# The input projections of a hybrid attention layer in five units of seven block products, with all of the attention half in one fixed list of steps

## The chip, the cores and the metric

The kernel runs on one core of a Trainium2 chip. A core has a matrix engine (TensorE, PE in the profile, with its weight loads as PEld), a vector engine (VectorE, DVE), an activation engine (ScalarE, ACT), GpSimd (POOL) and a queue engine (SyncE, SP), each with its own in-order queue of instructions, and 16 DMA engines between the chip's memory and the core's SBUF. TensorE writes its results to PSUM; the other engines read them there. Engines wait for each other by semaphores. The metric is the time of one execution on the device, in microseconds, as the median of several runs.

## The reference

One layer on 256 tokens of width 2048, in float32:

```
h    = rms_norm(x, attn_norm)
qa, ka, va, fa, qb, kb, vb = split(h @ w_in)     # 1024 each, fa 8 columns
qa, ka = rms_norm per head of 128
c    = cumsum(log_sigmoid(fa + b_forget))
out_a = softmax(qa ka^T / sqrt(128) + c_t - c_s, s <= t) va      # 8 heads
out_b = stick-breaking attention(qb, kb, vb), s < t               # 8 heads
x    = x + concat(rms_norm(out_a), rms_norm(out_b)) @ w_out
u    = causal conv of width 3 (rms_norm(x) @ w_up)                # 2 x 5632 columns
x    = x + (silu(gate half of u) * value half of u) @ w_down
```

Weights in all are some 200 MB, each used once, so every weight tile is loaded, prepared and used in one pass.

## The kernel before

Products keep float32 accuracy through a split. Of each operand a high part (`w_hi`, a cast on ACT, L208) and the rest (`w_lo`, a subtraction on DVE, L209) are made, and three products are summed: high by high, low of the tokens by high, high by low (`in_three`, L222 to L232, its matmul is L229). A weight piece is 2048 columns a partition: 4 tiles of 128 contraction rows by 512 columns, `w_raw`, 1 MB, loaded by SP.

The attention half is ordered by a scheduler that follows data and priorities. Ten projections of 512 columns read the normalised tokens `hT`: the forgetting heads' q and k, in two halves each (`project`, token-major, 4 pieces of 24 matmuls); the stick-breaking q and k in two halves each (`sb_heads`, feature-major, 16 pieces, L261 and L266); and the stick-breaking v in two halves. The forgetting heads' v and the 8 gate columns are three more projections of 344 columns. The first projection runs with the loading and the transposing of x (`opening`). Token-major q and k are turned into heads by transposes on TensorE (`ps_h`, L301) after a norm whose squares and sums are taken on DVE (`fox_rows`, L315, L317). The feature-major ones need no transposes, but the token factors `rstd1` in every partition (`pr`, L181). Heads are generators in a queue, `waiting`, of which each piece of a projection advances two. A head is a few small matmuls (`ps_s` or `ps_z`, `ps_p`, `ps_o`), exponentials on ACT, and masks and maxima on DVE. `w_out` is 16 pieces in two groups of 8, one for each kind of head; a column block of it is finished, added to x (L575), before the next begins. PSUM is in three pools of two: `psa` tiles of two banks, `psb` and `pss` of one.

The feed-forward half, from about 409 us on, is a list of steps in a fixed order, written out at the end of the function: at each step, weights for six steps ahead are loaded, those for four ahead summed, those for two ahead split, and the step's matmuls run. Its up-projection alternates with the down-projection of an earlier part; the down-projection takes seven block products in place of eight (`down_in_seven`), with banks `bank_a`, `bank_b` and `bank_c` as tiles of their own, and a buffer of its own for the sums of weights, `w_sum` (L781).

Of the kernel before, what the change touches and what calls it, by code (L numbers as in the profile page):

```python
# [14 lines left out]
P = 128  # L15
# [22 lines left out]
AHEAD = 200  # L38
WINDOW = 2
# [4 lines left out]
def hybrid_layer(  # L44
# [26 lines left out]

    const = ctx.enter_context(tc.tile_pool(name="const", bufs=1))
    big = ctx.enter_context(tc.tile_pool(name="big", bufs=1))
    small = ctx.enter_context(tc.tile_pool(name="small", bufs=4))
    psa = ctx.enter_context(tc.tile_pool(name="psa", bufs=2, space=bass.MemoryType.PSUM))
    psb = ctx.enter_context(tc.tile_pool(name="psb", bufs=2, space=bass.MemoryType.PSUM))

# [8 lines left out]
    x2 = big.tile([P, NT, D], F32, name="x2")  # L86
    xt = [x2[:, t, :] for t in range(NT)]
    xp = xf.rearrange("(t p) d -> p t d", p=P)

    def load_x(k, n):  # L90
        nc.sync.dma_start(x2[:, :, k * P : (k + n) * P], xp[:, :, k * P : (k + n) * P])

    with tc.high_priority(offset=AHEAD):
        load_x(0, 2)
        nc.sync.dma_start(cs[:, :P], cst[:, :P])
        nc.sync.dma_start(prow[:KT, :], attn_norm[0].rearrange("(n p) -> n p", p=P))
# [4 lines left out]
    ones = cs[:, C_ONE : C_ONE + P]  # L101

# [3 lines left out]
    def load_parameters(masks):  # L106
# [21 lines left out]


    pcol = const.tile([P, 50], F32, name="pcol")  # L130
    ga = const.tile([P, KT], F32, name="ga")
    g_ffn = pcol[:, KT : 2 * KT]
    g_fox, g_sb = pcol[:, 2 * KT : 2 * KT + NH], pcol[:, 2 * KT + NH : 2 * KT + 2 * NH]
    g_q, g_k = pcol[:, 48:49], pcol[:, 49:50]
# [6 lines left out]
    hT = big.tile([P, KT, 2, S], F32R, name="hT")  # L141

    def transposed_split(k, g):

        ps = psb.tile([P, 2, S], F32, name="ps_x", tag="t")
        for j in range(2):
            for t in range(NT):
                nc.tensor.transpose(  # L148
                    ps[:, j, t * P : (t + 1) * P], xt[t][:, (k + j) * P : (k + j + 1) * P], ident
                )  # L150
        for j in range(2):
# [7 lines left out]
    def sums_of_squares(ss, c):  # L159

        for t in range(NT):
            junk = late.tile([P, 512], F32, name="junk", tag="raw", bufs=4)
            act.activation(junk, xt[t][:, c * 512 : (c + 1) * 512], AF.Square, accum_out=ss[:, t, c : c + 1])

    def token_factors(ss, n):

        rstd = const.tile([P, NT], F32, name=f"rstd{n}")
        ssum = small.tile([P, NT], F32, name="ssum", tag="ssum")
        dve.tensor_reduce(ssum, ss, axis=AX.X, op=ALU.add)
        rsqrt(rstd, ssum, 1.0 / D, NT)  # L170
        dg = []
        for t in range(NT):
            dg.append(small.tile([P, P], F32, name="dg", tag="dg", bufs=2))
            dve.tensor_scalar(dg[t], ident, rstd[:, t : t + 1], None, op0=ALU.mult)
        return rstd, dg

    def in_every_partition(dg, n, pool):
        R = pool.tile([P, S], F32, name=f"R{n}")
        pr = psb.tile([P, S], F32, name="pr", tag="t")
        for t in range(NT):  # L180
            nc.tensor.matmul(pr[:, t * P : (t + 1) * P], ones, dg[t], start=t == 0, stop=t == NT - 1)  # L181
        dve.tensor_copy(R, pr)
        return R


    waiting = deque()

    def step():
        for g in list(waiting)[:WINDOW]:
            if next(g, g) is g:  # L190
                waiting.remove(g)

    def finish():
        while waiting:
            step()


    def load(src, into=None):
        raw = into if into is not None else wraw.tile([P, 2048], F32, name="w_raw", tag="w_raw")
# [15 lines left out]
    def weights(src, a, b):  # L215
        with tc.high_priority(offset=AHEAD):
            return split(load(src), a, b)

# [3 lines left out]
    def in_three(accs, parts, n, lhs, starts, stops):  # L222

# [3 lines left out]
        for j, (i, l, r) in enumerate(order):  # L227
            for t, o in enumerate(accs):
                nc.tensor.matmul(  # L229
                    o, lhs(i, l, t), r[:, i, :], start=starts and j == 0,  # L230
                    stop=stops and j == 3 * n - 1, skip_group_check=len(accs) == 1 and not starts,
                )  # L232

# [3 lines left out]
    def token_major(lhs, w, k0, nk, c0, cols, pieces=None, before=None):  # L237

        acc = psa.tile([P, NT, 512], F32, name="acc", tag="acc")
        k = 0  # L240
        for n in pieces or [4] * (nk // 4):
            if before:
                before(k, n)
            parts = weights(rows_of(w, k0 + k, n, c0, cols), n, cols)
            in_three(
                [acc[:, t, :cols] for t in range(NT)], parts, n,
                lambda i, part, t: of_half(lhs(k + i), part, t), k == 0, k + n == nk,
            )
            k += n
            step()  # L250
        return acc

    def feature_major(w, c0, pool, tag):

        acc = pool.tile([P, 2, 512], F32, name="pu", tag=tag)
        for kh in range(2):
            hi, lo = weights(rows_of(w, 8 * kh, 8, c0, 2 * P), 8, 2 * P)
            for i in range(8):
                k = 8 * kh + i
                for j in range(2):  # L260
                    nc.tensor.matmul(  # L261
                        acc[:, j, :], hi[:, i, j * P : (j + 1) * P],
                        hT[:, k].rearrange("p a b -> p (a b)"), start=k == 0, stop=False,
                    )
                for j in range(2):
                    nc.tensor.matmul(  # L266
                        acc[:, j, S:], lo[:, i, j * P : (j + 1) * P], hT[:, k, 0, :],
                        start=False, stop=k == KT - 1,
                    )
            step()  # L270
        return acc

    def summed(pool, acc, tag, **kw):

        t2 = pool.tile([P, 2, S], F32, name="t2", tag=tag, **kw)
        with tc.high_priority(offset=2 * AHEAD):
            act.copy(t2, acc[:, :, S:])
            dve.tensor_tensor(t2, acc[:, :, :S], t2, op=ALU.add)
        return t2

    with ExitStack() as actx:

        at = actx.enter_context(tc.tile_pool(name="at", bufs=1))
        pss = actx.enter_context(tc.tile_pool(name="pss", bufs=2, space=bass.MemoryType.PSUM))
        tmp = actx.enter_context(tc.tile_pool(name="tmp", bufs=2))
        wraw = actx.enter_context(tc.tile_pool(name="wraw", bufs=3))
        whi = actx.enter_context(tc.tile_pool(name="whi", bufs=2))
        wlo = actx.enter_context(tc.tile_pool(name="wlo", bufs=2))
        late = actx.enter_context(tc.tile_pool(name="late", bufs=1))

        def project(c0, cols, **kw):
            return token_major(lambda k: hT[:, k], wi, 0, KT, c0, cols, **kw)

        def scaled(dst, ps, t):
            act.activation(dst, ps, AF.Identity, scale=rstd1[:, t : t + 1])

        def to_heads(dst, rows, t, scale):

            ps = psb.tile([P, 4, P], F32, name="ps_h", tag="t")
            for h in range(4):  # L300
                nc.tensor.transpose(ps[:, h, :], rows[:, h * HD : (h + 1) * HD], ident)  # L301
            act.activation(dst[:, :, t * P : (t + 1) * P], ps, AF.Identity, scale=scale)

        def fox_rows(acc, dst, g):

            rows = []
            for t in range(NT):
                raw = late.tile([P, 512], F32, name="raw", tag="raw", bufs=4)
                scaled(raw, acc[:, t, :], t)
                rows.append(raw)  # L310
            for t in range(NT):
                raw = rows[t]
                r3 = raw.rearrange("p (h d) -> p h d", h=4)
                sq = late.tile([P, 512], F32, name="sq", tag="raw", bufs=4)
# [634 lines left out]
```

## Time and profile before

| | us |
|---|---|
| median of 3 runs | 1131.53 (1131.24 to 1132.13) |
| span of the profiled execution, first to last instruction | 1129.0 |
| TensorE busy | 1114.8 |
| VectorE busy | 843.3 |
| ScalarE busy | 680.6 |
| GpSimd busy | 20.9 |

The profiled execution's span lies 2.5 us under the median of the runs; what lies around it is not in the profile. In the rows quoted below, `L229` is line 229 of the kernel, `out<-in` are the program's tile names, and `xN` is a count. Matmuls are pipelined, so a group of them is read from its start to the next group's start. Of all the idle time, TensorE has 14 us, most of it at the two ends.

### The profile page before, as it was taken

Reading aid. Unit: us, or ns where it says so; the run is one execution under the profiler, and the core shown is the slowest. Engines: PE = TensorE matmul, PEld = TensorE weight load, DVE = VectorE, ACT = ScalarE, POOL = GpSimd, SP = SyncE. Lnnn points to the kernel's source line nnn. Section 1 sums busy time; section 2 is a strip of 40 time slices with the busy share of each in tenths; the row PEclk is TensorE's granted clock in tenths of the full one; section 3 lists DMA queues with packets and bytes.
Section 4 is the critical chain, followed back from the end, with each engine's and each line's share of the span. In section 5 each row is a group of like instructions: output and inputs, shape, how many; then the busy total and the mean of one; then the engine's idle time right before and its main releaser. Section 6 shows DMA issues by size and latency. Waiting matters only on the chain.

```text
span 1129.0 us, 14661 instructions
## 1 busy us (share of the span) xinstructions
PE 1114.8 (99%) x5890; PEld 956.6 (85%) x5890; DVE 843.3 (75%) x873; ACT 680.6 (60%) x840; POOL 20.9 (2%) x20
## 2 busy tenths in 40 slices
PE   7999999999999999999999999999999999999998
PEld 6998888888888888888888888888888888888886
DVE  4646656646556666766699898989989798989983
ACT  5644444445664566666667667766776667766751
POOL 0000000000000000000000000000000000000000
PEclk9999999999999999999999999999999999999999
DMA  7766555555444486555649697687949797696951
GB/s 234 219 206 218 171 158 159 185 159 178 149 149 150 149 256 199 188 190 192 195 144 252 220 268 249 187 265 195 290 149 242 240 252 242 188 288 182 291 172 66
DMA packets 170989, 228.17 MB, mean 202 GB/s; under 512 B 3992, under 2 KB 117802, under 8 KB 170922
## 3 DMA queue, kind: packets, MB, share of 16 engines
q1 hardware_dynamic: 162474, 210.47, 57.7%
q0 software_dynamic: 8448, 16.78, 8.6%
q8 instruction: 46, 0.75, 0.3%
q14 instruction: 21, 0.17, 0.0%
HBM read 225.14 MB, written 2.10 MB: 201 GB/s over the span
## 4 chain that ended last, share of the span: by engine, by line
PE 97%; DVE 1%; DMA 1%; ACT 0%; issue 0%; SPq 0%; DVEq 0%; ACTq 0%
PE pu L714 29%; PE acc L229 26%; PE pu L719 15%; PE bank_a L229 10%; PE pu L261 5%; PE bank_b L229 4%; PE pu L266 3%; PE bank_c L229 1%; DVE w_lo L209 1%; PE ps_x L148 1%; DMA x<-in_x_dram 0%; DMA w_raw<-in_w_up_dram 0%; PE ps_h L301 0%; ACT w_hi L208 0%; PE ps_z L511 0%
## 5 line engine op out<-in xcount | busy, mean ns | idle before, releaser
L209 DVE TENSOR_TENSOR w_lo<-w_raw,w_hi 128x2048 fp32r<-128x2048 f32 (+2 forms) x204 | 449.6, 2206 | 196.7 <-ACT w_hi L208 193.4
L208 ACT CAST w_hi<-w_raw 128x2048 fp32r<-128x2048 f32 (+2 forms) x204 | 376.0, 1843 | 248.5 <-PE acc L229 79.6
L714 PE MATMUL pu<-hT,w_hi 128*128 128x512 f32 x1408 | 441.7, 395 | 0.0
L719 PEld LDWEIGHTS pu<-hT,w_lo 128*128 128x128 f32 x1408 | 263.8, 188 | 65.8 <-DVE w_lo L209 4.6
L719 PE MATMUL pu<-hT,w_lo 128*128 128x256 f32 x1408 | 277.6, 278 | 0.9 <-DVE w_lo L209 0.9
L714 PEld LDWEIGHTS pu<-hT,w_hi 128*128 128x128 f32 x1408 | 218.8, 189 | 4.7
L229 PE MATMUL acc<-w_hi,hT 128*128 128x512 f32 (+1 forms) x640 | 143.3, 374 | 0.0
L229 PEld LDWEIGHTS acc<-w_hi,hT 128*128 128x128 f32 x640 | 114.2, 190 | 16.8
L261 PE MATMUL pu<-hT,w_hi 128*128 128x512 f32 x256 | 81.4, 399 | 0.0
L644 ACT ACTIVATE tap<-up,ccol 128x256 f32<-128x256 f32 x176 | 74.6, 495 | 0.0
L229 PE MATMUL acc<-w_lo,hT 128*128 128x512 f32 (+1 forms) x320 | 74.3, 371 | 0.0
L229 PEld LDWEIGHTS acc<-w_lo,hT 128*128 128x128 f32 x320 | 57.8, 189 | 8.7
L209 DVE TENSOR_TENSOR w_lo<-w_sum,w_hi 128x2048 fp32r<-128x2048 f32 x24 | 54.9, 2287 | 12.9 <-ACT w_hi L208 12.9
L208 ACT CAST w_hi<-w_sum 128x2048 fp32r<-128x2048 f32 x24 | 45.8, 1909 | 22.4 <-PE pu L714 20.0
L266 PEld LDWEIGHTS pu<-hT,w_lo 128*128 128x128 f32 x256 | 48.1, 188 | 11.4
L266 PE MATMUL pu<-hT,w_lo 128*128 128x256 f32 x256 | 50.4, 278 | 0.0
L229 PE MATMUL bank_a<-w_hi,g 128*128 128x512 f32 x192 | 47.0, 390 | 0.0
L229 PE MATMUL acc<-w_hi,oT 128*128 128x512 f32 x192 | 46.3, 393 | 0.0
L229 PEld LDWEIGHTS acc<-w_hi,oT 128*128 128x128 f32 x192 | 35.4, 188 | 7.0
L229 PEld LDWEIGHTS bank_a<-w_hi,g 128*128 128x128 f32 x192 | 34.5, 188 | 6.1
L261 PEld LDWEIGHTS pu<-hT,w_hi 128*128 128x128 f32 x256 | 39.0, 189 | 0.0
L637 ACT ACTIVATE gate<-up,ccol 128x256 f32<-128x256 f32 x44 | 24.0, 593 | 18.4 <-DVE up L630 18.4
(177 smaller groups left out, 1098.8 us busy)
## 6 DMA issues: line engine op xcount, KB each, us to landing
w_raw<-in_w_up_dram SPq DMA_DIRECT2D x88, 1024.0 KB, 9.9
w_raw<-in_w_down_dram SPq DMA_DIRECT2D x44, 1024.0 KB, 5.2
w_raw<-in_w_in_dram SPq DMA_DIRECT2D x36, 1024.0 KB, 5.3
w_raw<-in_w_out_dram SPq DMA_DIRECT2D x16, 1024.0 KB, 5.3
w_raw<-in_w_in_dram SPq DMA_DIRECT2D x12, 688.0 KB, 4.9
w_raw<-in_w_down_dram POOLq DMA_DIRECT2D x8, 1024.0 KB, 12.4
w_sum<-in_w_down_dram POOLq DMA_DIRECT2D x8, 1024.0 KB, 9.0
w_raw<-in_w_in_dram SPq DMA_DIRECT2D x8, 512.0 KB, 6.3
```

Of the source, the lines that this page charges most:

```text
L148: nc.tensor.transpose(ps[:, j, t * P : (t + 1) * P], xt[t][:, (k + j) * P : (k + j + 1) * P], ident)
L208: act.copy(hi[:, :n], raw[:, :n])
L209: dve.tensor_tensor(lo[:, :n], raw[:, :n], f32(hi[:, :n]), op=ALU.subtract)
L229: nc.tensor.matmul(o, lhs(i, l, t), r[:, i, :], start=starts and j == 0, stop=stops and j == 3 * n - 1, skip_group_check=len(accs) == 1 an ...
L261: nc.tensor.matmul(acc[:, j, :], hi[:, i, j * P : (j + 1) * P], hT[:, k].rearrange("p a b -> p (a b)"), start=k == 0, stop=False,)
L266: nc.tensor.matmul(acc[:, j, S:], lo[:, i, j * P : (j + 1) * P], hT[:, k, 0, :], start=False, stop=k == KT - 1,)
L637: act.activation(a[:, j, :], u[:, j, 2:], AF.Identity, scale=ccol[:, 2, f : f + 1], bias=ccol[:, 3, f : f + 1],)
L644: act.activation(taps[w][:, j, :], u[:, j, w : w + S], AF.Copy, scale=ccol[:, w, f : f + 1])
L714: nc.tensor.matmul(acc[:, j, :], hi[:, i, j * P : (j + 1) * P], hT[:, k].rearrange("p a b -> p (a b)"), start=k == 0, stop=False,)
L719: nc.tensor.matmul(acc[:, j, S:], lo[:, i, j * P : (j + 1) * P], hT[:, k, 0, :], start=False, stop=k == KT - 1,)
```

## The change

The attention half gets a list of steps too, and the two lists become one: every instruction of PE, DVE, ACT and SP in the whole kernel now stands in the order in which the list issues it. Lines here are those of the kernel after.

- **Opening and values.** The forgetting heads' v comes first: two blocks of 344 columns together, in 8 pieces with the loading of x (`opening`), then the third block in 4 (`last_values`), followed by the gates.
- **Five units.** The ten projections of 512 columns go in pairs, two column blocks n = 0 and 1 to a unit: A and B the forgetting q and k, C the stick-breaking q and k of the first half, V the stick-breaking v, D the q and k of the second half. With two token blocks t = 0 and 1, a unit has four results. For the first 1024 rows of the contraction it takes seven products of blocks in place of eight, 12 matmuls each, on sums of token blocks (made once, `token_sums`) and on sums of weight blocks (two by DVE, two by accumulating DMAs on POOL). For the other 1024 rows it takes four plain pieces of 24. That makes 11 steps. Its four PSUM banks are two tiles: `acc_ac` holds banks a and c, `acc_be` holds b and e. Partial results leave the banks several times in a unit, scaled by `rstd1` (evictions on ACT, L516 and L535; additions on DVE, L522).
- **Heads.** All q and k rows are token-major now, with transposes for the stick-breaking ones. The squares of the forgetting rows move from DVE to ACT: 16 activations of 128 columns with a sum (L577), eight to a tick.
- **x** gives its place to the token sums and is loaded a second time by four DMAs on POOL (`reload_x`) during unit D.
- **w_out.** The second group begins with the first halves of two column blocks, then their second halves.
- **Pools.** Five raw, three high and three low weight buffers throughout; `w_sum` is gone, as the sums are made in place.

The unit:

```diff
+    def unit(c_first, c_second, dst, done):
...
+            def matmuls():
+                if name == "a" and new:
+                    acc = acc_tile("acc_ac")
+                    bank["a"], bank["c"] = acc[:, 0, :], acc[:, 1, :]
+                if name == "b" and new:
+                    acc = acc_tile("acc_be")
+                    turn[0] ^= 1
+                    bank["b"], bank["e"] = acc[:, 0, :], acc[:, 1, :]
+                in_three([bank[name]], parts, 4, lhs, new, True)
...
+        def evict(name, n, t, negative=False):
+            def follow():
+                if not out:
+                    out.update(dst())
+                act.activation(out[n, t], bank[name], AF.Identity, scale=r(t, negative))
+                yield
...
+        def finish():
+            act.activation(out[0, 1], bank["a"], AF.Identity, scale=r(1))
+            yield
+            add("c", 0, 0)
+            yield
+            yield from done(out)
+
+        product("a", True, of_raw(0, 0), "11", [("11", w11)], follow=evict("a", 0, 0))
+        product("c", True, of_raw(1, 0), "21", [("21", w21)])
+        product("b", True, of_sums(T5), "11", [("12", w12)], sum_of("12"), follow=evict("b", 1, 1))
+        plain(1, 0, [(1, "e"), (0, "b")])
+        product("a", False, of_sums(S2), "11", [("22", w22)], sum_of("22"), follow=evict("a", 1, 0, True))
+        plain(1, 1, [(1, "e"), (0, "b")], then_add(("e", 1, 1)))
+        product("a", False, of_sums(T7), "12", plus=w22, follow=then_add(("a", 1, 1, True)))
+        product("b", False, of_sums(S4), "22", follow=then_add(("b", 1, 0)))
+        plain(0, 0, [(0, "c"), (1, "a")])
+        product("a", False, of_raw(1, 1), "11", plus=w21)
+        plain(0, 1, [(1, "a"), (0, "c")], finish)
```

The squares, the order of `w_out` and the list's loop:

```diff
-                dve.tensor_tensor(sq, raw, raw, op=ALU.mult)
...
-                dve.tensor_reduce(ss, sq.rearrange("p (h d) -> p h d", h=4), axis=AX.X, op=ALU.add)
...
+            for m, nt in enumerate(order):
+                for h in range(4):
+                    act.activation(
+                        junk[:, :HD], rows[nt][:, h * HD : (h + 1) * HD], AF.Square,
+                        accum_out=ss[:, m, h : h + 1],
+                    )
+                if m % 2:
+                    yield
...
+    for c in range(4):
+        for kh in range(2):
+            out_rows(0, c, kh)
+    for c, kh in ((0, 0), (1, 0), (0, 1), (1, 1), (2, 0), (2, 1), (3, 0), (3, 1)):
+        out_rows(1, c, kh)
...
     for n in range(-LOAD, len(steps) + 8):
...
+        at_step(LOAD, 0)
+        advance(following)
+        at_step(SPLIT, 2)
+        advance(following)
+        advance_heads()
+        at_step(SUM, 1)
+        at_step(0, 3)
+        advance(after)
+        advance_heads()
```

More of the change, by code (lines that the diff above doesn't have):

```diff
@@ L157, in transposed_split, with squares @@
             )
-    def sums_of_squares(ss, c):
+    def squares(ss, c):
         for t in range(NT):
[L162 to L167, printed above, removed]
+            act.activation(
+                junk, x2[:, t, c * 512 : (c + 1) * 512], AF.Square, accum_out=ss[:, t, c : c + 1]
+            )
@@ L168, in token_factors @@
+    def token_factors(rstd, ss):
         ssum = small.tile([P, NT], F32, name="ssum", tag="ssum")
         dve.tensor_reduce(ssum, ss, axis=AX.X, op=ALU.add)
[L170 to L183, printed above, removed]
@@ L186, in hybrid_layer @@
[L186 to L199, printed above, removed]
+        yield from rsqrt(rstd, ssum, 1.0 / D, NT)
+    steps, following, after, waiting, running = [], [], [], deque(), []
+    hooks = {}
+    ticks = [0, -STAGGER]
@@ new lines, in hybrid_layer, with new_step, advance, advance_heads @@
+    turn = [0]
+    def new_step(load, sums, prepare, matmuls, follow=None):
+        steps.append((load, sums, prepare, matmuls, follow))
+    def advance(tasks):
+        tasks[:] = [g for g in tasks if next(g, g) is not g]
+    def advance_heads():
+        ticks[0] += 1
+        if waiting and ticks[0] - ticks[1] >= STAGGER:
+            running.append(waiting.popleft())
+            ticks[1] = ticks[0]
+        advance(running)
+    def acc_tile(name, slot=None):
+        if slot is None:
+            slot = turn[0]
+            turn[0] ^= 1
+        return psa.tile([P, 2, 512], F32, name=name, tag=f"acc{slot}")
@@ L200, in load @@
+    def load(src):
+        raw = wraw.tile([P, 2048], F32, name="w_raw", tag="w_raw")
         a, b = src.shape[1:]
@@ L234, in of_half, with of_tokens, pieces, loads @@
     def of_half(h, part, t):
         return h[:, part, t * P : (t + 1) * P]
[L237 to L244, printed above, removed]
+    def of_tokens(k0):
+        return lambda i, part, t: of_half(hT[:, k0 + i], part, t)
+    def pieces(w, k0, n, c0, cols, matmuls, follow=None):
+        mem = {}
+        def loads():
+            mem["raw"] = load(rows_of(w, k0, n, c0, cols))
+        def prepare():
+            mem["parts"] = split(mem["raw"], n, cols)
+        new_step(loads, None, prepare, lambda: matmuls(mem["parts"]), follow)
@@ new lines, in sb_rows, with done, start_sb, value_rows @@
+    def sb_rows(half):
+        def done(rows):
+            while started["fox"] < NH or started["sb"] < 4 * half:
+                yield
+            yield from to_heads(rows, (f"qB{half}", f"kB{half}"), (QSCALE, 1.0))
+            ready.add(f"qB{half}")
+            if "vB" in ready:
+                start_sb(half)
+        return done
+    ready = set()
+    def start_sb(half):
+        for h in range(4 * half, 4 * half + 4):
+            waiting.append(sb_head(h, half))
+    def value_rows():
+        tile_of["vB"] = row_tiles("vB")()
+        return tile_of["vB"]
@@ new lines, in norm_of_heads @@
+    def norm_of_heads(group, rg):
+        pg = psb.tile([P, NT], F32, name="pg", tag="t")
+        for t in range(NT):
+            nc.tensor.matmul(
+                pg[:, t : t + 1], ssq[group][:, t * P : (t + 1) * P], ones[:, 0:1],
+                start=t == 0, stop=t == NT - 1,
+            )
+        yield
+        yield from rsqrt(rg, pg, 1.0 / WF, NT)
+        ready.add(f"rg{group}")
+    rgs = [const.tile([P, NT], F32, name=f"rg{i}") for i in range(2)]
+    rstd2 = const.tile([P, NT], F32, name="rstd2")
@@ new lines, in next_rows, with rows_split, out_rows, matmuls @@
+    def next_rows(c):
+        pairs = [(k, transposed(k)) for k in (4 * c, 4 * c + 2)]
+        following.append(rows_split(pairs))
+        yield
+    def rows_split(pairs):
+        for k, ps in pairs:
+            split_tokens(ps, k, g_ffn)
+            yield
+    cells = {}
+    def out_rows(group, c, kh):
+        def matmuls(parts):
+            if kh == 0:
+                cells[c] = acc_tile("acc_o")
+            if group == 1 and kh == 1:
+                while waiting or running:
+                    advance_heads()
+            heads = [hT[:, 4 * kh + i] for i in range(4)] if group == 0 else oSb[4 * kh : 4 * kh + 4]
@@ new lines, in matmuls, with follow @@
+                lambda i, p, t: of_half(heads[i], p, t), kh == 0, kh == 1, middle=middle,
+            )
+            if kh == group and c == 0:
+                following.append(norm_of_heads(group, rgs[group]))
+        def follow():
+            acc = cells[c]
+            while f"rg{group}" not in ready:
+                yield
+            for t in range(NT):
+                xs = x2[:, t, c * 512 : (c + 1) * 512]
+                dve.scalar_tensor_tensor(
+                    xs, acc[:, t, :], rgs[group][:, t : t + 1], xs, op0=ALU.mult, op1=ALU.add
+                )
+            if group == 1:
+                after.append(next_rows(c))
+                yield
+                squares(ss2, c)
+                if c == 3:
+                    for _ in token_factors(rstd2, ss2):
+                        pass
+                    for t in range(NT):
+                        dg2.append(small.tile([P, P], F32, name="dg", tag="dg"))
+                        dve.tensor_scalar(dg2[t], ident, rstd2[:, t : t + 1], None, op0=ALU.mult)
@@ L606, in parameters @@
         dve.tensor_copy(ccol, pc)
-    steps = []
-    def new_step(load, sums, prepare, matmuls, follow=None):
-        steps.append((load, sums, prepare, matmuls, follow))
     class Part:
```

834 lines of the change are left out of this document (464 added, 370 removed).

## The prediction

> **What bounds the kernel now.** I read the page first (engines, chain), then the waits of TensorE, then the windows.
>
> ```profile
> span 1129.0 us, 14661 instructions
> PE 1114.8 (99%) x5890; PEld 956.6 (85%) x5890; DVE 843.3 (75%) x873; ACT 680.6 (60%) x840; POOL 20.9 (2%) x20
> ...
> PE 97%; DVE 1%; DMA 1%; ACT 0%; issue 0%; SPq 0%; DVEq 0%; ACTq 0%
> ```
> ```profile
> PE pp L138 <- DMA prow<-in_attn_norm_dram: 4.3, 1, 4.3
> PE ps_x L148 <- DMA x<-in_x_dram: 2.8, 1, 2.8
> ```
> ```profile
> 0.00:9.00 9.00, 1.90 (x8) 1.52 (x9) 1.17 (x4) 3.12 (x4) 0.20 (x4) 1.00 0.69 211
> ...
> 36.00:131.00 95.00, 94.86 (x515) 85.90 (x515) 54.38 (x75) 47.25 (x59) 0.00 (x0) 1.00 0.64 202
> 131.00:281.00 150.00, 150.00 (x833) 130.08 (x831) 93.05 (x143) 72.83 (x107) 0.00 (x0) 1.00 0.55 168
> 281.00:398.00 117.00, 117.00 (x573) 98.88 (x572) 68.60 (x80) 67.37 (x94) 0.00 (x0) 1.00 0.44 145
> 398.00:430.00 32.00, 30.84 (x171) 26.21 (x171) 22.98 (x32) 17.22 (x25) 0.00 (x0) 1.00 0.93 288
> ```
>
> The windows give stretch, its length, busy time of PE, weight load, DVE, ACT and POOL, granted clock, DMA share, GB/s. TensorE bounds: the chain is PE for 97%, and from 36 to 398 us, where the change lies, it loses 0.14 us. Its only long waits are in the first 9 us. DVE and ACT are busy for 62% and 49% in the middle window, so they have room, and DMA moves 145 to 202 GB/s where 288 is also seen. Less TensorE work there is a gain one to one, if nobody makes TensorE wait.
>
> **TensorE's work.** Rows of its timeline (start, us, what); a duration there overlaps its neighbour, so I take start to start.
>
> ```profile
> 105.79 3.79 PE L229 MATMUL acc<-w_hi,hT 128*128 128x512 f32 x16
> ...
> 111.23 3.79 PE L229 MATMUL acc<-w_hi,hT 128*128 128x512 f32 x16
> ...
> 116.68 0.60 PE L301 MATMUL ps_h<-cs,raw 128*128 128x128 f32 x4
> 117.03 1.18 PE L229 MATMUL acc<-w_hi,hT 128*128 128x512 f32 x4
> ...
> 156.18 0.63 PE L261 MATMUL pu<-hT,w_hi 128*128 128x512 f32 x2
> ...
> 160.35 0.63 PE L261 MATMUL pu<-hT,w_hi 128*128 128x512 f32 x2
> ...
> 601.84 1.99 PE L229 MATMUL bank_b<-w_hi,s 128*128 128x512 f32 x8
> ...
> 604.57 0.61 PE L714 MATMUL pu<-hT,w_hi 128*128 128x512 f32 x2
> ...
> 610.37 2.00 PE L229 MATMUL bank_a<-w_hi,s 128*128 128x512 f32 x8
> ```
>
> A piece of 24 matmuls of 512 columns takes 5.44 us; a feature-major piece is eight groups of (160.35 − 156.18)/6 = 0.695, 5.56 us; a product of 12 takes 2.73; four matmuls of 128 columns 0.35. The first v keeps its matmuls (other pieces, the same count of 344 columns). Of the other ten projections, before: q0, k0, q1, k1 of 4 pieces, 16 × 5.44 = 87.0; the second v 8 × 5.44 = 43.5; the second q and k 16 × 5.56 = 89.0; in all 219.5 us. After: five units of seven products and four plain pieces, 5 × (7 × 2.73 + 4 × 5.44) = 204.4. That is −15.1. The second q and k now need transposes, 8 groups of 0.35 = +2.8, and `pr` for rstd1, four matmuls, goes, −0.4. **Sum of TensorE's work: −12.7 us.** w_out and the feed-forward half keep their matmuls.
>
> **What waits in the new order.** ACT's and DVE's instructions now run in the order in which the list of steps issues them. These are the durations (count | busy, mean ns):
>
> ```profile
> L209 DVE TENSOR_TENSOR w_lo<-w_raw,w_hi 128x2048 fp32r<-128x2048 f32 x184 | 420.7, 2288 | 171.3 <-ACT w_hi L208 170.9
> ...
> L208 ACT CAST w_hi<-w_raw 128x2048 fp32r<-128x2048 f32 x184 | 351.5, 1910 | 226.4 <-PE pu L714 67.8 <-PE acc L229 64.8 <-issue 53.7
> ...
> L575 DVE SCALAR_TENSOR_TENSOR x<-acc,rg,x 128x512 f32<-128x512 f32 x16 | 11.8, 747 | 12.0 <-PE acc L229 11.9
> ...
> L295 ACT ACTIVATE raw<-acc,rstd 128x512 f32<-128x512 f32 x8 | 5.0, 681 | 0.0
> ```
> ```profile
> 132.29 0.37 ACT L455 ACTIVATE pr<-ps_s,nm 128x128 f32<-128x128 f32 x1 [2.32 <-DVE nm L451]
> 132.56 0.19 ACT L455 ACTIVATION_READ_ACCUMULATOR pr<-ps_s,nm 128x1 f32 x1
> 132.65 0.47 ACT L456 ACTIVATE pr<-ps_s,nm 128x256 f32<-128x256 f32 x1
> 133.01 0.20 ACT L456 ACTIVATION_READ_ACCUMULATOR pr<-ps_s,nm 128x1 f32 x1
> 133.29 1.91 ACT L208 CAST w_hi<-w_raw 128x2048 fp32r<-128x2048 f32 x1
> ```
>
> Cast 1.9, subtraction 2.3, eviction 0.68, scaled add 0.75, a head's pair of exponentials 1.0. A fox row's square (L577 after) is an activation of 128 columns with a sum: 0.27 + 0.19 from the rows at 132.29 and 132.56, and as all share `junk` each waits for the one before, so about 0.48; eight of a tick 3.9 us (2.9, at the 0.36 from 132.29 to 132.65, if they overlap).
>
> Two things make TensorE wait. Banks a and c are halves of one PSUM tile, b and e of another, and waits go by tile: product 1 (c) may not start before ACT has evicted product 0's a, though that is another bank; plain step 3 (e) waits in the same way for b. And the steps are short: before, a product of 2.73 had 5.80 us of other matmuls behind it (604.57 to 610.37); now product follows product. ACT can't run ahead, for the last eviction of a unit (L535) waits for the unit's last matmul. Zero in each chain is that moment:
>
> - A→B, product 1: ACT evicts (0.7), casts step 2's weights (to 2.6), squares (to 6.5), evicts a (to 7.1); TensorE is through with product 0 at 2.7. **4.4.** Step 3: eight more squares, a cast and the small ACT steps of the norm stand before b's eviction. **3.2.**
> - B→C: the exponentials of head 3 wait for DVE's mask and maxima behind a subtraction and an add (8.9; before, ACT waited 2.3 for such maxima at 132.29), then eight squares (12.8), the eviction (13.5); TensorE, with the head's matmuls, is there at 5.8. **7.7.** Head 3's transposes wait for DVE behind the next subtraction: **2.3.**
> - C→V: no squares; exponentials again late (7.75), then an eviction, a cast (10.3), and the copy of the transposed rows (11.0) for whose PSUM buffer the next transposes wait; TensorE comes at 5.4. **6.0.**
> - V→D, step 3: ACT has a sum's cast, a head's `sps` behind DVE's two subtractions (13.5), and b's eviction (14.2); TensorE comes at 9.9. **4.3.**
> - Last values→A, product 1: ACT has vA, a cast and the gates' three activations behind DVE's `lf`, which is behind a subtraction. **4.4.**
> - Products 6 to 8 of each unit: product 7 (b) waits for DVE's add from e, which is behind the subtraction for step 8: cast 1.9 + 2.3 + 0.75 + handoffs = 5.1 after step 5's last high matmul, TensorE 0.9 + 2.73 = 3.6. 1.5 each, **7.5** in five units.
> - w_out, second group: (0,1) and (1,1) end one after the other, so the third tile waits for the sums of column block 0, behind a cast that waits for step (1,1), its subtraction, four small operations and two adds: 9.9 after (0,1), TensorE 5.4. **4.5.** Then 16 transposes share two PSUM buffers, each emptied by alternate ACT and DVE work: **3.2.**
>
> These are 47.5 us. Shorter ones (gates' `pc` 2.0, two evictions 0.7 and 1.4, B's transposes 1.5 and 1.2, C's 1.0, a second `sps` 1.4) come to 9.2; such small ones may vanish in the ones before, I count half, 4.6.
>
> **At nothing**, with its cover: the loads (10 MB a unit in 41 us and the waits, at most 250 GB/s, within the 288 of the windows; five raw buffers); x's reload (2 MB, issued some 24 us before its first use); DVE's sums and `token_sums` (if DVE lost its room, 2.3 each); w_sum's buffer, saved in the feed-forward half; the opening, bound by x as now (±1).
>
> **Sum.** Profiled span 1129.0, median of runs 1131.5: 2.5 outside. 1131.5 − 12.7 + 47.5 + 4.6 = 1170.9. **I forecast 1171 us, slower by 3.5%.** Bounds of this case: with half of the long chains caught up, 24 less, 1147; with all of the small waits (4.6 more) and a third more of the long ones (16), 1192.
>
> **Two pages weighed.** The granted clock stayed 1.00 in the first 9 us, with waits of 4.3 and 2.8. The Trainium skill, "TensorE: Matmul & The Clock Gate", "What's actually happening", says that an idle window of some 3.4 us halves the clock until about 3.4 us of activity have passed; six waits of that length would by this page cost an estimated 1.7 each, 10 us more, 1181. The trace of before doesn't show it, and I leave it out. The same waits turn on this rule of "Perfetto Trace Analysis", "Optimizing Tensor Performance": groups that rotate through different PSUM banks let the evacuation of one overlap the next. By it a and c would not wait for each other, which is the first rival below; no run here shows yet which holds.
>
> **Rivals.**
> - *Evictions in time (the other side).* If waits went by bank, and evictions overtook the squares, TensorE would stay the bound as in 36 to 398 us: 1131.5 − 12.7 = 1119. For it: DVE and ACT have 38% and 51% of room there. Against it: the room is a mean, and the fixed order puts eight squares and a cast ahead. It decides where the waits in all stay under 12.7. 0.07.
> - *Only the longest count.* Product 1 of A, B and C, step 3 of D and w_out's 4.5 hold, 25 us, and the rest is caught up in them: 1144. For it: while TensorE waits, ACT and DVE catch up. Against: each unit begins a new chain at its own end. 0.12.
> - *DVE and ACT become the bound.* In a fox unit with its heads DVE has 13 × 2.3 + 4 × 0.75 + rows and heads of 14, 47 us, ACT about 45, in 49 of TensorE; each in-order wait then adds to the next: over 1192. 0.08.
> - *Equal:* waits of 10 to 15 us by chance. 0.02.
>
> **Chances.** Mine 0.71 (1147 to 1192). About 0.2% is what a measurement of this kernel can tell from no change: faster 0.08, same 0.02, slower 0.90. The range 1140 to 1192 leaves out the first and the third rival.
>
> **What would show it.** TensorE's busy time some 13 us less, and its waits led by "acc_ac <- ACT" and "acc_be <- ACT" with single ones of 4 to 8 us; DVE's adds at L522 next; waits of `ps_x` and `acc_o` in w_out; no waits on DMA beyond the opening; the feed-forward half unchanged. I am wrong if the evictions run within a microsecond of their products, or if DMA or the opening carries the loss.

## The result, and the profile after

The changed kernel takes 1204.25 us (median of 4 runs, 1203.65 to 1204.84), the kernel before beside it 1131.38: a ratio of 1.064, with a 95% interval of 1.063 to 1.066. It is slower, as forecast, but by nearly twice as much, and outside the range. The page of the kernel after begins like this (engines with busy time, share and count; then the granted clock in 40 slices of 30 us):

```profile
span 1203.0 us, 14455 instructions
...
PE 1131.8 (94%) x5730; PEld 957.4 (80%) x5730; DVE 894.1 (74%) x849; ACT 726.5 (60%) x914; POOL 36.6 (3%) x34
...
PEclk9989998889989998999999999999999999999999
```

TensorE has 160 instructions less, and yet is busy for 17.0 us more (1131.8 against 1114.8), and idle for 71.2 us where it was idle for 14.2, 57.0 more. Together that is the 74.0 us by which the span grew. By the forecast's prices there are 12.7 us less of work, and the busy time is 17.0 longer: the matmuls that are left took 29.7 us longer than those prices say. The clock's dips all lie in the first 16 slices, that is, up to 480 us. The feed-forward half is what it was: its first matmul starts at 482.7 us instead of 409.4, 73.3 later, and from there to the end it is 720.3 us against 719.6.

TensorE's waits in the kernel after (waiting tile, whom it waited for, us in total, times, the longest):

```profile
PE ps_p L667 <- DVE pr L662: 8.8, 4, 3.9
PE acc_ac L250 <- ACT rA L516: 7.1, 1, 7.1
PE acc_ac L250 <- ACT rC L516: 6.7, 1, 6.7
PE acc_o L250 <- ACT junk L188: 4.7, 1, 4.7
PE ps_h L566 <- ACT qB L568: 4.4, 2, 4.1
...
PE acc_ac L250 <- ACT rB L516: 3.8, 1, 3.8
...
PE acc_be L250 <- ACT rD L516: 3.6, 1, 3.6
PE ps_z L710 <- DVE sps L706: 3.2, 2, 2.9
```

TensorE waits for no DMA beyond the opening. ACT's timeline before product 1 of unit C shows such a wait from the other side (start, us, what, idle before it):

```profile
178.13 0.69 ACT L535 ACTIVATE rB<-acc_ac,rstd 128x512 f32<-128x512 f32 x1 [0.32 <-PE acc_ac L250]
178.72 1.90 ACT L232 CAST w_hi<-w_raw 128x2048 fp32r<-128x2048 f32 x1
180.51 0.48 ACT L670 COPY pT<-ps_p 128x384 f32<-128x384 f32 x1
184.63 0.37 ACT L657 ACTIVATE pr<-ps_s,nm 128x128 f32<-128x128 f32 x1 [3.63 <-DVE nm L652]
...
185.44 0.31 ACT L577 ACTIVATE junk<-rB 128x128 f32<-128x128 f32 x1
...
188.78 0.67 ACT L516 ACTIVATE rC<-acc_ac,rstd 128x512 f32<-128x512 f32 x1
```

It is the chain of the prediction: the unit's last eviction, a cast, 3.6 us idle until DVE has the head's maxima, the exponentials, eight squares from 185.44 to 188.78, and only then the eviction that TensorE waits for. What follows on TensorE is not in the forecast (product 1 of unit A):

```profile
70.85 3.78 PE L250 MATMUL acc_ac<-w_hi,hT 128*128 128x512 f32 x8 [7.12 <-ACT rA L516]
74.43 1.45 PE L250 MATMUL acc_ac<-w_lo,hT 128*128 128x512 f32 x4
75.72 0.59 PE L411 MATMUL pc<-cs,lrep 128*128 128x256 f32 x2
```

Eight matmuls take 3.58 us (70.85 to 74.43), where eight take 1.82 at the usual pitch (two thirds of the 2.73 for twelve). The granted clock of that stretch says so too (columns as in the prediction's windows; the third row is the part of the second in which the clock is at half):

```profile
40.00:60.00 20.00, 20.00 (x126) 19.50 (x125) 16.32 (x22) 13.95 (x18) 0.00 (x0) 1.00 0.56 182
60.00:80.00 20.00, 12.11 (x44) 8.91 (x42) 17.71 (x16) 8.86 (x13) 2.22 (x2) 0.83 0.88 258
68.38:75.21 6.83, 4.36 (x10) 3.47 (x11) 5.85 (x8) 3.56 (x6) 0.00 (x0) 0.50 1.07 238
```

Between 68 and 468 us the trace has ten such stretches at 0.50, each 3.4 or 6.8 us long, 51.2 us in all. Eight of them lie at the eight single waits of 3.6 us or more beyond the opening, one at the wait of 2.9 (`ps_z`, 348.87), and one behind two waits of 1.7 and 2.2 in w_out. A stretch begins between 2.5 us ahead of the wait's end and 1.5 us behind it. TensorE is busy in them for 43.3 us; at half the clock half of that is lost, an estimated 21.6 us of the 29.7. Where the other 8 us went isn't shown.

The trace of before had a sign of it, in its first matmuls of 512 columns, which follow idle times of 4.3 and 2.8 us with little work between (two rows of the timeline, then the window of the first):

```profile
9.15 3.76 PE L229 MATMUL acc<-w_hi,hT 128*128 128x512 f32 x8
12.71 1.15 PE L229 MATMUL acc<-w_lo,hT 128*128 128x512 f32 x3
```
```profile
9.15:12.71 3.56, 3.56 (x11) 2.79 (x10) 3.20 (x5) 1.78 (x3) 0.00 (x0) 1.00 0.91 306
```

3.56 us for eight, though the granted clock of that window is 1.00. The trace's record of the clock begins only at 13.33 us (13.77 in the kernel after), and a window ahead of that reads 1.00 because nothing is on record there. The matmuls' own pitch tells a slow clock at the start, the column can't.

### The profile page after: what moved, and what is told of

Its sections match the earlier page's. It is cut to its first block, busy times and chain, and to the rows that moved or that the text cites. A ratio compares the mean times of both kernels' runs of the same rounds, so it can differ in the third digit from the quotient of the medians.

```text
span 1203.0 us, 14455 instructions
## 1 busy us (share of the span) xinstructions
PE 1131.8 (94%) x5730; PEld 957.4 (80%) x5730; DVE 894.1 (74%) x849; ACT 726.5 (60%) x914; POOL 36.6 (3%) x34
## 4 chain that ended last, share of the span: by engine, by line
PE 63%; DVE 2%; ACT 1%; issue 0%; DVEq 0%; ACTq 0%
PE pu L943 26%; PE pu L948 13%; PE bank_a L250 9%; PE acc_o L250 5%; PE bank_b L250 4%; PE acc L250 3%; DVE w_lo L233 1%; PE bank_c L250 1%; ACT w_hi L232 1%; DVE xb L962 0%; ACT hT L180 0%; DVE hT L181 0%; PE ps_x L172 0%; PE ps_o L719 0%; DVE xb L797 0%
## 5 line engine op out<-in xcount | busy, mean ns | idle before, releaser
L233 DVE TENSOR_TENSOR w_lo<-w_raw,w_hi 128x2048 fp32r<-128x2048 f32 (+1 forms) x239 | 537.2, 2253 | 225.7 <-ACT w_hi L232 225.6
L232 ACT CAST w_hi<-w_raw 128x2048 fp32r<-128x2048 f32 (+1 forms) x239 | 448.9, 1879 | 226.6 <-PE pu L943 90.0
L943 PE MATMUL pu<-hT,w_hi 128*128 128x512 f32 x1408 | 441.9, 395 | 1.7 <-DVE hT L181 1.7
L948 PEld LDWEIGHTS pu<-hT,w_lo 128*128 128x128 f32 x1408 | 263.8, 188 | 65.1 <-DVE w_lo L233 3.9
L948 PE MATMUL pu<-hT,w_lo 128*128 128x256 f32 x1408 | 277.5, 278 | 0.7 <-DVE w_lo L233 0.6
L250 PE MATMUL acc_ac<-w_hi,hT 128*128 128x512 f32 x280 | 79.9, 433 | 17.6 <-ACT rA L516 7.1
L250 PEld LDWEIGHTS acc_ac<-w_hi,hT 128*128 128x128 f32 x280 | 57.1, 210 | 30.8 <-ACT rA L516 7.6
L250 PE MATMUL acc_o<-w_hi,hT 128*128 128x512 f32 x192 | 49.1, 406 | 0.0
L250 PE MATMUL acc_be<-w_hi,hT 128*128 128x512 f32 x160 | 42.2, 408 | 5.4 <-ACT rD L516 3.6
L250 PE MATMUL acc_ac<-w_lo,hT 128*128 128x512 f32 x140 | 40.7, 415 | 0.1
```

What stands on the lines that cost most here:

```text
L232: act.copy(hi[:, :n], raw[:, :n])
L233: dve.tensor_tensor(lo[:, :n], raw[:, :n], f32(hi[:, :n]), op=ALU.subtract)
L250: nc.tensor.matmul(o, lhs(i, l, t), r[:, i, :] if cut is None else r[:, i, cut], start=starts and j == 0, stop=stops and j == 3 * n - 1, s ...
L943: nc.tensor.matmul(acc[:, j, :], hi[:, i, j * P : (j + 1) * P], hT[:, k].rearrange("p a b -> p (a b)"), start=k == 0, stop=False,)
L948: nc.tensor.matmul(acc[:, j, S:], lo[:, i, j * P : (j + 1) * P], hT[:, k, 0, :], start=False, stop=k == KT - 1,)
```

## The experiments

A *tick* below is a turn in which the list's loop lets each waiting piece of work go on to its next `yield` (for most of them two turns in a step); one `yield` more puts what follows it one turn later. Each run changes the kernel after unless it says otherwise, and differences are to its 1204.25 us. Theory at first: TensorE waits because waits go by PSUM tile and stand behind ACT's and DVE's fixed order; each long wait brings slow matmuls. Rivals: ACT's and DVE's load sets the pace; the fixed list does.

**Each bank a tile.** In the attention half, `acc_ac` and `acc_be` become two tiles each.

```diff
-        return psa.tile([P, 2, 512], F32, name=name, tag=f"acc{slot}")
+        if not in_ffn:
+            return Banks([psa.tile([P, 512], F32, name=name, tag=f"acc{slot}{j}") for j in range(2)])
+        return psa.tile([P, 2, 512], F32, name=name, tag=f"acc{slot}")
```

> Each PSUM bank of the attention half is a tile of its own, nothing else changes. Theory (waits go by tile): the waits before product 1 of A, B and C (7.1, 3.8, 6.7 us), before step 3 of A, B and D (0.8, 0.8, 3.6) and before product 7 (1.4, 1.4, 1.0) go, 27 us, and with the four long ones some 8 us of slow matmuls behind them: about 1170 us. Rival (ACT and DVE in their fixed order are the bound, a wait taken away comes back at the next place): 1195 to 1204 us, with larger waits of ps_p, ps_h and w_lo.

1201.59 us, 2.7 less than the kernel after and on the rival's side. Its waits:

```profile
PE ps_p L678 <- DVE pr L673: 17.2, 5, 8.2
PE ps_z L721 <- DVE sps L717: 8.1, 2, 4.1
PE pc L422 <- issue: 7.1, 1, 7.1
```

The edit does what it says: the waits for ACT's evictions before products 1 are gone. But `pc` now waits 7.1 us where product 1 of A did, and the transposes of head 3 8.2 us where product 1 of C did. (For `pc` the profile names no releaser; DVE's copies into `lrep`, which `pc` reads, start at 75.39 us, and `pc` at 75.72, where it also starts in the kernel after.) TensorE gets further by one product and then meets the same late ACT and DVE. Tiles are where it stood, and by themselves hardly why.

**The squares a tick later.** One more `yield` ahead of the squares in `fox_rows`.

> The squares of the fox rows start one tick later, behind the eviction of bank a instead of ahead of it; the PSUM tiles stay as they are. Theory (what stands ahead of the eviction on ACT sets the wait): product 1 of B waits under 1 us instead of 3.8, product 1 of C about 3 instead of 6.7 (the exponentials stay ahead of it), 7 us, and 2 to 4 us of slow matmuls: about 1194 us. Rival (ACT's load sets the wait, whatever the order): 1204 us.

1209.18 us, 4.9 more, where the theory had 10 less and the rival no change. Product 1 of B waits 0.8 us, of C 3.4, as the theory has it; but the squares now stand ahead of b's eviction, and step 3 of B waits 8.0. The order on ACT decides, and this order is no better.

**Both.**

> Both edits. Theory: with banks as tiles no product waits for an eviction, so the place of the squares hardly matters any more: 1165 to 1172 us, within 5 us of the banks alone. Rival (load of ACT and DVE): as the banks alone or not below 1195 us.

1212.81 us, 11.2 more than the banks alone. That is far from the theory; it is above the rival's 1195, but that it would be worse than the banks alone was in neither. `acc_be` waits 6.4 us for b's eviction in B, and the row transposes of B 4.5 us.

**The waits filled.** 26 and 12 matmuls on `hT` into a spare bank, in TensorE's waits before product 1 of A and of B.

```diff
+                if name == "c" and fill[0]:
+                    n_fill = fill.pop(0)
+                    spare = psb.tile([P, 512], F32, name="spare", tag="t")
+                    for j in range(n_fill):
+                        nc.tensor.matmul(
+                            spare, hT[:, 0, 0, :P], hT[:, 0].rearrange("p a b -> p (a b)"),
+                            start=j == 0, stop=j == n_fill - 1,
+                        )
```

> The kernel after, with 26 and 12 matmuls on hT into a spare PSUM buffer (their result is not used) in TensorE's waits before product 1 of A and of B, some 5.9 and 2.7 us of 7.1 and 3.8. Theory (a TensorE that was idle for some 3.5 us runs at half speed for its first 2 to 4 us): the waits end at the same time and the eight matmuls behind them take 2.0 us instead of 3.8 and 2.5: 3 to 4 us less, about 1200.5 us. Rival (the slow matmuls come from their operands or from PSUM, not from the idle time): the rows stay slow and the time at 1204 us or above.

1204.50 us, no change. In TensorE's timeline at A:

```profile
64.19 6.07 PE L496 MATMUL spare<-hT 128*128 128x512 f32 x26
71.47 2.11 PE L250 MATMUL acc_ac<-w_hi,hT 128*128 128x512 f32 x8 [1.22 <-ACT rA L525]
73.43 1.08 PE L250 MATMUL acc_ac<-w_lo,hT 128*128 128x512 f32 x4
75.94 0.70 PE L411 MATMUL pc<-cs,lrep 128*128 128x256 f32 x2 [1.44 <-DVE lrep L406]
```

Behind a filled wait the eight matmuls take 1.96 us (71.47 to 73.43): the idle time makes them slow, not their operands. That agrees with what the Trainium skill says in "TensorE: Matmul & The Clock Gate", "What's actually happening", of a clock halved after an idle window. Yet the time won is lost at once: `pc` now waits 1.44 us for DVE and starts at 75.94 us instead of 75.72, and in B step 3 waits 2.0 us instead of 0.8 for b's eviction and starts at 129.68 instead of 129.69. At these two places the slow matmuls cost nothing in the end, since what comes next is late anyway.

**Plain units.** Two projections of four pieces in place of the eleven steps, in the same list; x's reload and the splits of the forgetting heads' output are moved to fit the shorter unit D.

> The kernel after, in the same list, but each unit is two plain projections of four pieces of 24 matmuls in place of the eleven steps: no block products, no sums of weights, one eviction of each bank. TensorE's work grows by 5 x 2.73 = 13.6 us. Theory (in a unit ACT and DVE have 11 casts, 11 subtractions, 2 sums and 8 evictions or adds, each waiting for the other in the fixed order, for 41 us of TensorE; a plain unit has 8 and 8 for 43.5): most of the 40 us of waits and of the 15 to 20 us of slow matmuls within the units go: 1157 to 1172 us. Rival (the fixed order of the list costs the time, whatever a step is): 1195 us or more.

1182.20 us, between the two: 22 us less than the kernel after with 13.6 us more of TensorE's work. So the block products cost 36 us of waits and slow matmuls (by the profiles 20.8 of idle time and 15.1 of slower matmuls), more than they save; but the list without them is still 50 us slower than the kernel before.

**w_out in the order of column blocks.**

```diff
-    for c, kh in ((0, 0), (1, 0), (0, 1), (1, 1), (2, 0), (2, 1), (3, 0), (3, 1)):
+    for c, kh in ((0, 0), (0, 1), (1, 0), (1, 1), (2, 0), (2, 1), (3, 0), (3, 1)):
```

> The kernel after with the second group of w_out in the order of column blocks, (0,0), (0,1), (1,0), (1,1) and so on. Theory (the third PSUM tile waits for the add of the first column block, which ends late in the order after): the wait of 4.7 us and the 1.6 us of slow matmuls behind it go, and part of the 3.9 us of the transposes: 1196 to 1199 us. Rival (DVE's backlog there is the cause, the wait comes back at the next tile): 1203 to 1205 us.

1195.47 us, 8.8 less, a little more than the theory had; the wait of 4.7 is gone and does not come back.

**Exponentials and scalings of the fox heads (the forgetting ones) one tick later.** Two `yield` lines more in `fox_head`.

> The kernel after; a forgetting head takes its exponentials and its scaling one tick later each, so that ACT's casts stand ahead of activations that wait for DVE, and DVE's subtractions ahead of those that wait for ACT. Theory (the alternation of ACT and DVE in the fixed order sets the pace of B and C): the waits of ps_p (3.9 twice, 0.5 twice) and part of the 6.7 us before product 1 of C go, with their slow matmuls: 1188 to 1196 us. Rival (the load of DVE and ACT sets it): 1203 us or more.

1190.05 us, 14.2 less, as the theory has it. The long `ps_p` waits fall to 1.8 at most and the 6.7 us before product 1 of C to 0.5.

**Slack.** The last two with two ticks more ahead of the gates' `pc` and of the first row transposes, and one ahead of the second transposes and of the suffix sums: with banks as tiles, without, and on plain units.

> The kernel after with each PSUM bank a tile, w_out in the order of column blocks, the fox head's late exponentials and scalings, and one to two ticks more ahead of four TensorE instructions that follow DVE or ACT work: the gates' pc, the first row transposes, the second transposes after a copy, the stick-breaking head's suffix sums. Theory (the list places TensorE instructions right behind work that alternates between ACT and DVE; a wait taken away comes back at the next such place, unless all of them get slack): 1150 to 1162 us. Rival (ACT's and DVE's load in a unit is the bound, whatever the placing): 1172 us or more.

> The same without the banks as tiles. Theory: the waits that go by tile stay (7.1, 3.8, 3.6 and the 0.8 to 1.4 ones, 20 us, with some 6 us of slow matmuls), the others go: 1172 to 1182 us, 15 to 25 us above the run with the banks, where the banks alone gave 2.7. Rival (the tiles don't matter): within 5 us of it.

> Plain units (no block products, 13.6 us more of TensorE's work than the kernel after) with w_out in the order of column blocks and the same slack. Theory: of the 1182.2 us of the plain units the waits of ps_p, ps_h, ps_z and w_out go (some 27 us with their slow matmuls): 1150 to 1158 us. Rival (the fixed list loses against data-driven order anyway): 1170 us or more.

1178.37, 1184.35 and 1152.52 us. With slack the banks are worth 6.0 us, not the 15 to 25 expected. The plain units do what the theory says: 29.7 us less than the plain units above, which had neither slack nor the new order of w_out. The block units do not: 1178.37 lies on the side of the rival, load whatever the placing. On the same footing but for the tiles they are 26 us slower with 13.6 us less work. Their longest waits, and those of the plain units:

```profile
PE ps_z L729 <- DVE sps L724: 10.7, 3, 4.7
PE ps_p L685 <- DVE pr L680: 5.6, 3, 2.6
PE pc L424 <- DVE lrep L417: 4.2, 1, 4.2
```
```profile
PE ps_s L675 <- DVE cRh L669: 5.7, 4, 2.4
...
PE ps_z L744 <- DVE sps L739: 3.5, 3, 2.3
```

**Less DVE work, and more TensorE work,** on the kernel after. The first leaves the ten sums of weight blocks out. The second adds four matmuls behind each product, into the same bank. Neither computes the layer any more.

> The kernel after without the ten sums of weight blocks on DVE (2.3 us each, 23 us); the products take the unsummed blocks, so this part of the computation is left out. TensorE, ACT and the loads do the same work. Theory (in the units the pace is set by DVE's and ACT's work in its fixed order, DVE's share of it above all): 1182 to 1192 us. Rival (TensorE's own path with single waits for ACT sets it, DVE has room): 1199 to 1204 us.

> The kernel after with four more matmuls of 512 columns behind each block product, into the same bank (they add a part twice, which the reference doesn't): 35 x 0.91 = 31.8 us more of TensorE's work, nothing else. Theory (TensorE has room in the units, ACT and DVE set the pace): at most 12 us more, up to 1216 us, the waits of TensorE falling by 20 us or more. Rival (the time is TensorE's work plus its waits, the sum of the forecast): 1228 to 1236 us, with the same waits.

1200.84 and 1225.99 us. 22 us less of DVE's busy time give 3.4: the wait at A falls from 7.1 to 4.8 us, those at B and C stay at 3.8 and 6.8. So DVE's load isn't the bound of the units. At A it counts: in the kernel after a sum of weights and two subtractions stand on DVE right ahead of the gates' `lf`:

```profile
62.52 2.29 DVE L508 TENSOR_TENSOR w_raw<-w_raw 128x2048 f32<-128x2048 f32 x1
64.72 4.49 DVE L233 TENSOR_TENSOR w_lo<-w_raw,w_hi 128x2048 fp32r<-128x2048 f32 x2
69.13 0.35 DVE L386 SCALAR_TENSOR_TENSOR lf<-acc_v,rstd,bf 128x8 f32<-128x8 f32 x2
```

31.8 us more of TensorE's work cost 21.7: neither theory's number, but nearer to the sum of work and waits. A third of the added work went into time in which TensorE had waited:

```profile
PE ps_p L671 <- DVE pr L666: 8.0, 2, 4.0
PE acc_ac L250 <- ACT rA L520: 6.2, 1, 6.2
PE acc_ac L250 <- ACT rC L520: 5.9, 1, 5.9
```

The longest waits stay, a little shorter; B's falls to 2.9 us and D's to 1.4. My reading is that each starts at an event of TensorE's own (the end of a unit, a head's matmuls) and goes round through ACT and DVE, so that it is a matter of how long the round is and less of how full an engine is. No run takes work off ACT alone, so ACT's share of it isn't shown.

**A fourth buffer for w_hi.** ACT's waits in the kernel after name one more part of the round: within 60 to 440 us its casts (`w_hi`) wait for TensorE to free one of the three buffers.

```profile
ACT pr L657 <- DVE nm L652: 30.4, 8, 5.0
ACT w_hi L232 <- PE acc_be L250: 24.9, 11, 3.1
...
ACT w_hi L232 <- PE acc_ac L250: 17.3, 10, 3.6
```

Narrower tiles make room for a fourth; they are the control.

> A control for the next run, to make room in SBUF: the kernel after with the fox heads' outputs and the transposed q and k kept in bfloat16 (less exact than the reference). Both theories: 1202 to 1205 us, at most a microsecond or two less for shorter head matmuls.

> The control with a fourth buffer for w_hi in the attention half. Theory (with three buffers a cast waits for the end of the step three before it, 42 us of ACT's time in the units, and what stands behind it on ACT and DVE is late by that): 8 to 20 us less than the control, the casts' waits for TensorE mostly gone. Rival (the alternation of ACT and DVE makes the lateness, and a cast that waits has nothing urgent behind it): within 3 us of the control.

> The control on top of the kernel with banks as tiles, slack and w_out in the order of column blocks: both theories 1176 to 1179 us.

> That one with the fourth buffer. Theory (buffers): with the placing out of the way they count more, 12 to 22 us less than its control, 1155 to 1166 us. Rival (alternation): within 4 us of its control.

1202.64 and 1193.99 us: 8.7 less, the low end of what the theory expected. The casts' waits for `acc_be` and `acc_ac` fall from 41.9 us in the control to 12.5, but TensorE's before product 1 of A, B and C stay at 7.1, 3.7 and 6.9. With slack, 1176.21 and 1173.57: 2.6 less, as the rival has it. The buffers are a part of the lateness where nothing else gives slack, and little beside it.

**Further ticks** ahead of `ps_s`, `ps_p`, `ps_o`, the suffix sums and `pc`.

> The kernel with banks as tiles and slack, with one more tick ahead of ps_s, ps_p, ps_o and the suffix sums, and two more ahead of the gates' pc, where its longest remaining waits stand (4.2, 4.0, 4.7, 2.6, 2.6 us). Theory (placing: every wait is a TensorE instruction too close behind ACT and DVE): 1158 to 1168 us. Rival (in a block unit ACT and DVE have no room left, waits move on once more): 1173 us or more.

> The same further ticks with plain units. Theory (placing): of the 9 us of waits behind the opening most go, with their slow matmuls: 1141 to 1147 us, some 10 to 15 above the kernel before. Rival: 1150 us or more.

The block units came to 1168.58 us (runs from 1165.7 to 1172.0), 9.8 less and 0.6 above what placing would give; the plain ones to 1150.00, 2.5 less and on the rival's side. In the block units the waits had moved again:

```profile
PE ps_z L713 <- ACT w L740: 6.1, 4, 2.6
PE ps_s L661 <- ACT pr L678: 5.6, 4, 3.6
```

No version tried beats the kernel before; the nearest, plain units, is 18 us behind it. How much of the 37 us that are left to the block units is placing, and how much can't be had in units so short, stays open.

## Why the prediction was right and wrong

- **What bounds the kernel, TensorE's work.** Right. Products and pieces run at 2.73 and 5.44 us where nobody waits, and the feed-forward half is unchanged.
- **What waits in the new order.** The kind of wait was right, and the sum came close: 52.1 us counted, 57.0 measured. That it came so close is in part luck, as single terms were off both ways: of the 47.5 us of named chains some 39 came, and waits that weren't named, or only among the small ones, made up for the rest. Product 1 of A 7.1 instead of 4.4: a sum of weights, which the forecast had at nothing, stands on DVE ahead of `lf`, and without the sums the wait is 4.8. Product 1 of B 3.8 for 4.4, of C 6.7 for 7.7; step 3 of B 0.8 for 3.2; eight squares 3.3 for 3.9; V's transposes 4.1 for 6.0; step 3 of D 3.6 for 4.3; product 7 only 1.4, 1.4 and 1.0 us instead of 1.5 in each of five units; w_out 4.7 for 4.5. The 3.9 us of each half's first head before `ps_p`, twice, weren't foreseen, though the chain is the one worked out for head 3.
- **"Such small ones may vanish, I count half."** Counted in full they would have brought the sum to 56.7, beside 57.0 measured; but it was in the main other waits that came.
- **"The trace of before doesn't show it, and I leave it out."** This is the step that failed, the weighing of the clock. It was priced at 10 us by the page of the Trainium skill that the prediction cites, and set to nothing by the granted clock's column of the first 9 us, where the trace has no record of the clock. In the sum of the prediction a term is missing: the matmuls took 29.7 us longer, an estimated 21.6 of them at half the clock at ten places. Twice the page's price came because ten places had it and not six, and because the stretches were up to 6.8 us long. The two matmul rows at 9.15 and 12.71 of the trace of before hinted at it. With it the span adds up, 1129.0 − 12.7 + 57.0 + 29.7 = 1203.0; as the 29.7 is what was left over, that is a balance and no test. Nor would fast matmuls alone have given the time back: where two of the waits were filled, the matmuls were fast and the time was the same. The late ACT and DVE come first, the slow clock is what their waits bring with them.
- **Banks and tiles as the cause.** The waits by tile are there, but they aren't the cause: with banks as tiles 2.7 us went, not 27, and 6.0 where there was slack. The rule of "Perfetto Trace Analysis" in the Trainium skill, that groups in different banks let one's evacuation overlap the next, holds in that run for the products themselves; it changes little where ACT and DVE are late for what comes next.
- **The rivals.** Evictions in time: no, the eviction at 188.78 stands where the chain put it. Only the longest count: no, the waits were there in full. DVE and ACT as the bound, over 1192: its time is the nearest to what came, but not its mechanism, since DVE's work could fall by 22 us with 3.4 to show for it; for ACT's load no run settles it. That a wait taken away turns up at the next place, close to its "each in-order wait then adds to the next", is what the runs bear out.
- **DMA, the opening, x's reload, w_sum.** Right, at nothing. DVE's sums, also at nothing, cost something: without them the kernel is 3.4 us shorter, and the wait at A 2.3.

## What to carry to other kernels

When work leaves the engine that bounds, ask what the others must do in the shorter steps: here the products saved 13.6 us and cost 36 in waits and slow matmuls, because each step needs the same cast and subtraction in half the time, and evictions beside, in an order that can't bend. Before trusting a wait's named releaser, ask what the waiting engine would meet next: the waits that went with the tiles were worth 2.7 us of 27, as the next thing was late too, while the one wait of w_out, with nothing late behind it, was worth 8.8 with what hung on it, and slack at several places at once was worth more. Price an idle TensorE at more than the idle time, by the pitch of the matmuls behind an idle stretch that the trace already has, but expect that part back only if what comes next is in time. And before a granted clock of 1.00 is taken as a measurement, check it against the pitch of the matmuls.

## What was not expected of the hardware

Behind a wait of 7.1 us TensorE's matmuls ran at half pace, eight in 3.58 us instead of 1.82, and filling the wait with other matmuls brought them to 1.96. The clock was at half in ten stretches of 3.4 or 6.8 us, behind waits of 2.9 us and more or two of 1.7 and 2.2 close together. From 9.15 to 12.71 us of the kernel before, the granted clock's column read 1.00 while eight matmuls took 3.56 us; the record of the clock begins at 13.33.
